# Tree attention on one core: GpSimd's V copies placed behind the next group's V loads, and stores eight groups of four heads behind the loads in place of twelve

## The chip, the core and the metric

The kernel runs on one core of a Trainium2 chip. The core has a matrix engine (TensorE, called PE in the profile), three engines for elementwise work (VectorE or DVE, ScalarE or ACT, GpSimd or POOL), an engine that mostly issues transfers (SyncE or SP), and 16 DMA engines that move data between the device memory and the core's memory SBUF. TensorE writes into a small accumulator memory, PSUM. Each engine works off its own list of instructions in order and waits on semaphores for the others.

The metric is the device time of one execution in microseconds. Beside it stands the span of a profiled execution, from its first instruction to its last, which is shorter by what lies around it.

## What is computed

```python
batch, heads, seq, dim = 8, 12, 512, 64
mask[i, i] = 1                      # and 1 at every ancestor of i
parent = i
while parent > 0:
    parent = (parent - 1) // 2
    mask[i, parent] = 1
scores = einsum('bhqd,bhkd->bhqk', Q, K) / sqrt(dim) + (1 - mask) * (-1e9)
weights = exp(scores - max(scores)); weights /= sum(weights) + 1e-10
out = einsum('bhqk,bhkd->bhqd', weights, V)
```

Each of the 512 positions is a node of a binary tree and attends to itself and to its ancestors only. There are 96 heads in all (8 x 12). Q, K, V and the output are float32, 12.58 MB each.

## The kernel before

**Tiles.** Node n = 4p + t lies in partition p, slot t. A head is then 128 partitions x 4 slots x 64 numbers. The heads are worked on at three grains: a *group* `o` of eight heads is loaded at once (12 groups, `NO`); a *pair* `i` of two heads is computed at once (48 pairs, `NP`, four to a group); four heads, a *quad* `q`, are stored at once (24 of them, `NQ`, two to a group).

**Loads.** All loads are issued by GpSimd and turn float32 into bfloat16 on the way. `load_k` and `load_q` bring the group's K and Q (line 179). `load_v_tiles(o)` issues four transfers of V: partitions 64 to 127 to a staging tile `vst`, two transfers that put partitions 32 to 63 straight into the value tile `vt` (line 197), and partitions 0 to 31 to `vst`. K, Q and `vst` have four buffers each, `vt` has four as well (`NV`).

**V's spreading.** The value tile wants rows in another order than V has them. `spread_top` (line 203) makes four copies on GpSimd, each 32 partitions by eight heads; `spread_leaves` and `spread_l7` (lines 217 and 230) copy on VectorE. `values` cannot begin with a group before its copies are made.

**A pair's way.** `transpose(i)` turns K and Q on TensorE (line 253); `evac` copies them to SBUF on VectorE (line 279). `scores1` and `scores2` multiply Q by the keys of the tree's top and of the lower parts (lines 290 to 321), with mask codes added by matmuls, and ScalarE takes the exponentials. `values(i)` multiplies by V with a column of ones beside it (line 341), and `norm(i)` divides by the sums on VectorE (lines 367 and 370) into the output tile `of[q]`. The loop over i (line 445) runs scores of pair i, values of pair i - 1, transposes of pair i + 2.

**The order on GpSimd.** It is written out by hand in `pool_program` (line 387), a generator that the main loop steps through. For groups 0 and 1 there is a start of its own with smaller loads. From group 2 on, each round issues K and Q of group o, makes the copies of group o - 1, issues V of group o, and then the two stores `2 * o - BEHIND` and the one after it, if there are such. `BEHIND` is 12, so stores begin in the round of group 6 and the last round's are quads 10 and 11. Behind the last round come the copies of group 11 and then the stores of quads 12 to 22. The last quad is stored in three pieces: two by SyncE, one by ScalarE. The stepping (line 457) settles in which order the program is written down, not when an instruction runs: GpSimd runs its list in order, held by semaphores alone. A store waits for `norm` of its two pairs. The output tiles have 15 buffers.

Of the kernel before, what the change touches and what calls it, by code (L numbers as in the profile page):

```python
# [103 lines left out]
def kernel(  # L104
# [70 lines left out]
    def load(kept, name, pool, src, o, h0=0, n=8, rows=(0, 128)):  # L175

        if o not in kept:
            kept[o] = pool.tile([P, 8, 4, D], bf16, name=name)
        nc.gpsimd.dma_start(  # L179
            out=kept[o][rows[0]:rows[1], h0:h0 + n, :, :].rearrange("p h t d -> p h (t d)"),  # L180
            in_=src[rows[0]:rows[1], 8 * o + h0:8 * o + h0 + n, :],
        )

    def load_k(o, h0=0, n=8):
        load(ksts, "kst", loads, Kr, o, h0, n)

    def load_q(o, h0=0, n=8):
        load(qsts, "qst", loads, Qr, o, h0, n)

    def load_v(o, *args):  # L190
        load(vsts, "vst", vloads, Vr, o, *args)

    def load_v_tiles(o):

        load_v(o, 0, 8, (64, 128))
        for half in range(2):
            nc.gpsimd.dma_start(
                out=vts[o % NV][32 * half:32 * half + 32, :, VCOL[1]:VCOL[1] + 2 * D],
                in_=Vr[32:64, 8 * o:8 * o + 8, 2 * D * half:2 * D * half + 2 * D],
            )  # L200
        load_v(o, 0, 8, (0, 32))

    def spread_top(o, h0=0, h1=8):
        for j in range(4):
            nc.gpsimd.tensor_copy(  # L205
                out=vts[o % NV][32 * j:32 * j + 32, h0:h1, VTOP:VTOP + D],
                in_=vsts[o][0:32, h0:h1, UNITS[TOP + j][1], :],
            )
# [168 lines left out]
    def store(eng, q, h0=0, n=4):  # L377
        eng.dma_start(  # L378
            out=Or[:, 4 * q + h0:4 * q + h0 + n, :],
            in_=ofs[q][:, h0:h0 + n, :, :].rearrange("p h t d -> p h (t d)"),  # L380
        )


    BEHIND = 12
    NO = NQ // 2

    def pool_program():

        for h0 in (0, 2):
            load_k(0, h0, 2)  # L390
            load_q(0, h0, 2)
        load_v(0, 0, 4)
        load_k(0, 4, 4)
        load_q(0, 4, 4)
        load_v(0, 4, 4)
        load_k(1, 0, 4)
        load_q(1, 0, 4)
        spread_top(0, 0, 4)
        load_v_tiles(1)
        load_k(1, 4, 4)  # L400
        load_q(1, 4, 4)
        spread_top(0, 4, 8)
        yield
        yield
        for o in range(2, NO):
            load_k(o)
            load_q(o)
            spread_top(o - 1)
            load_v_tiles(o)
            yield  # L410
            for q in (2 * o - BEHIND, 2 * o + 1 - BEHIND):
                if q >= 0:
                    store(nc.gpsimd, q)
        spread_top(NO - 1)
        for q in range(NQ - BEHIND, NQ - 1):
            yield
            store(nc.gpsimd, q)
# [17 lines left out]
    def pool_until(done, wanted):  # L435
        while done < wanted:
            next(program, None)
            done += 1
        return done

    program = pool_program()
    steps = pool_until(0, 1)
    transpose(0)
    evac(0)
    for i in range(NP + 1):
# [13 lines left out]
        else:  # L459
            steps = pool_until(steps, min(steps + 2, NO + (i - 2) // 2 - (NQ - 1 - BEHIND)))  # L460
        if i == NP - 1:
# [33 lines left out]
```

## Time and profile before

| what | value |
|---|---|
| time, three runs | 151.35, 151.4, 153.65 us; median 151.4 us |
| time of the profiled execution | 149.99 us |
| its span | 148.2 us |
| mean granted TensorE clock | 0.925 |
| busy: PE, DVE, ACT, POOL | 109.7, 96.0, 84.6, 101.7 us |
| chain of waits: PE, DVE, issue, DMA | 57%, 18%, 12%, 3% of the span |

How to read it: the profile lists instructions by line of the kernel, with their engine, operation and tiles (`vt<-vst` is a copy from the staging tile to the value tile). A time in brackets behind a row of the timeline is how long the engine had been idle, and what ended that. Rows by stretch of time give each engine's busy time and, in the last three columns, TensorE's granted clock, the DMA engines' share and the rate that they moved. The DMA share can pass 1 since the times of overlapping packets are added.

### The profile page before, as it was taken

How to read it: one execution, taken by the hardware profiler on the slowest of the kernel's cores; microseconds unless marked ns; L12 is line 12 of the kernel's file. 1: busy time of each engine (PE TensorE's matmuls, PEld its weight loads, DVE VectorE, ACT ScalarE, POOL GpSimd, SP SyncE). 2: the span in 40 equal slices, each digit the busy share in tenths (PEclk: the TensorE clock that was granted, in tenths of full speed). 3: DMA queues.
4: the chain of work that ended last, by engine and by line, in shares of the span. 5: the costliest groups of instructions: out<-in, count | busy, mean ns of one | idle time of the engine just before them, and what ended most of it. 6: DMA issues, size and time to landing. Idle time of an engine off the chain costs nothing.

```text
span 148.2 us, 5852 instructions
## 1 busy us (share of the span) xinstructions
PE 109.7 (74%) x2592; PEld 81.4 (55%) x2592; DVE 96.0 (65%) x205; ACT 84.6 (57%) x98; POOL 101.7 (69%) x155
## 2 busy tenths in 40 slices
PE   0486798988989999598689969679798697962000
PEld 0245585766867757476457747556576475741000
DVE  3037699796896987677835957748867859752000
ACT  4044258685886777667727748584586757680000
POOL 7949979449597595977975946966976907992000
PEclk9998579999999999999969999999999999998555
DMA  4999999999999999999999999999999994799993
GB/s 130 148 159 195 192 194 200 190 198 133 160 193 186 172 168 157 177 208 308 198 199 329 203 223 313 197 246 281 192 244 284 197 250 182 240 311 326 339 351 145
DMA packets 44938, 32.30 MB, mean 218 GB/s; under 512 B 7280, under 2 KB 41840, under 8 KB 44912
## 3 DMA queue, kind: packets, MB, share of 16 engines
q0 software_dynamic: 44208, 30.94, 122.4%
q1 hardware_dynamic: 560, 0.85, 1.8%
q8 instruction: 20, 0.33, 0.8%
q10 hardware_dynamic: 144, 0.13, 0.3%
q14 instruction: 6, 0.05, 0.1%
HBM read 38.21 MB, written 12.58 MB: 343 GB/s over the span
## 4 chain that ended last, share of the span: by engine, by line
PE 57%; DVE 18%; issue 12%; DMA 3%; ACT 1%; POOL 1%; ACTq 0%; POOLq 0%
PE ob L341 21%; PE kqp L253 13%; PE s L290 8%; PE s L295 5%; PE s L321 5%; DVE of L370 5%; PE s L312 4%; DVE kq L279 4%; DVE vt L217 3%; DMA qst<-in_Q_dram 3%; DVE vt L239 2%; DVE rec L367 2%; DVE vt L230 2%; POOL kst L179 1%; ACT e L326 1%
## 5 line engine op out<-in xcount | busy, mean ns | idle before, releaser
L301 ACT ACTIVATE e<-s 128x1024 bf16<-128x1024 f32 x48 | 49.2, 1024 | 44.8 <-PE s L295 43.9
L205 POOL COPY vt<-vst 32x512 bf16<-32x512 bf16 (+1 forms) x52 | 31.2, 600 | 24.9 <-DMA vst<-in_V_dram 20.7
L341 PE MATMUL ob<-vt,e 128*128 128x65 bf16 (+1 forms) x960 | 40.0, 200 | 9.2 <-issue 4.8
L326 ACT ACTIVATE e<-s 128x768 bf16<-128x768 f32 x48 | 38.6, 805 | 2.7 <-PE s L321 2.7
L341 PEld LDWEIGHTS <-e 128*128 128x128 bf16 (+1 forms) x960 | 31.5, 104 | 15.0 <-issue 6.7
L279 DVE COPY kq<-kqp 128x1024 bf16<-128x1024 bf16 x48 | 32.7, 682 | 10.1 <-PE kqp L253 10.0
L370 DVE TENSOR_TENSOR of<-ob,rec 128x512 f32<-128x512 f32 x48 | 33.2, 691 | 1.7
L253 PE MATMUL kqp<-ctile,kst 128*64 128x128 bf16 x384 | 20.8, 231 | 7.5 <-DMA kst<-in_K_dram 5.4
L367 DVE RECIPROCAL rec<-ob 128x8 f32<-128x8 f32 x48 | 9.9, 207 | 25.3 <-PE ob L341 24.5
L321 PEld LDWEIGHTS <-kq 64*128 64x128 bf16 x576 | 17.0, 96 | 10.6 <-issue 5.9
L253 PE MATMUL kqp<-ctile,qst 128*64 128x128 bf16 x384 | 20.6, 231 | 1.6 <-issue 1.3
L321 PE MATMUL s<-kq 64*128 64x96 bf16 (+2 forms) x576 | 18.3, 191 | 4.1 <-issue 4.1
L290 PE MATMUL s<-ctile 64*128 64x512 bf16 x96 | 19.8, 400 | 1.2 <-issue 1.1
L295 PE MATMUL s<-kq 64*128 64x512 bf16 x96 | 19.2, 392 | 0.7 <-DVE kq L279 0.7
L378 POOL DMA_DIRECT2D out_dram<-of x23 | 17.5, 769 | 1.4 <-issue 1.4
L253 PEld LDWEIGHTS <-kst 128*64 128x64 bf16 x384 | 13.8, 117 | 8.0 <-DMA kst<-in_K_dram 5.4
L179 POOL DMA_DIRECT2D qst<-in_Q_dram x15 | 12.8, 854 | 6.1 <-DMA qst<-in_Q_dram 2.3
L312 PE MATMUL s<-ctile 64*128 64x384 bf16 x96 | 16.8, 335 | 0.2
L253 PEld LDWEIGHTS <-qst 128*64 128x64 bf16 x384 | 14.9, 118 | 2.0 <-issue 1.4
L179 POOL DMA_DIRECT2D vst<-in_V_dram x24 | 15.9, 661 | 0.0
L179 POOL DMA_DIRECT2D kst<-in_K_dram x15 | 13.1, 873 | 0.8 <-POOLq L479 0.8
L217 DVE COPY vt<-vst 64x1024 bf16<-64x1024 bf16 (+1 forms) x26 | 12.8, 493 | 0.8
(15 smaller groups left out, 42.6 us busy)
## 6 DMA issues: line engine op xcount, KB each, us to landing
out_dram<-of POOLq DMA_DIRECT2D x23, 512.0 KB, 7.5
kst<-in_K_dram POOLq DMA_DIRECT2D x10, 512.0 KB, 8.4
qst<-in_Q_dram POOLq DMA_DIRECT2D x10, 512.0 KB, 10.0
vst<-in_V_dram POOLq DMA_DIRECT2D x13, 256.0 KB, 6.3
vt<-in_V_dram POOLq DMA_DIRECT2D x22, 64.0 KB, 6.1
vst<-in_V_dram POOLq DMA_DIRECT2D x11, 128.0 KB, 6.2
kst<-in_K_dram POOLq DMA_DIRECT2D x3, 256.0 KB, 6.9
qst<-in_Q_dram POOLq DMA_DIRECT2D x3, 256.0 KB, 7.5
```

The lines of the kernel that those rows point to most:

```text
L179: nc.gpsimd.dma_start(out=kept[o][rows[0]:rows[1], h0:h0 + n, :, :].rearrange("p h t d -> p h (t d)"), in_=src[rows[0]:rows[1], 8 * o + h0 ...
L205: nc.gpsimd.tensor_copy(out=vts[o % NV][32 * j:32 * j + 32, h0:h1, VTOP:VTOP + D], in_=vsts[o][0:32, h0:h1, UNITS[TOP + j][1], :],)
L253: nc.tensor.transpose(out=dst, in_=st[i // 4][:, 2 * (i % 4) + a, t, :], identity=perm)
L279: nc.vector.tensor_copy(out=kq[:, :, :, :].rearrange("p k (x y) c -> p k x (y c)", x=2), in_=src)
L290: nc.tensor.matmul(out=sp[:, a, :], lhsT=k1code[64 * a:64 * a + 64, :], rhs=q1code[64 * a:64 * a + 64, :], start=True, stop=False,)
L295: nc.tensor.matmul(out=sp[:, a, :], lhsT=keys(i, a, TOP), rhs=qTs[i][64 * a:64 * a + 64, :, :].rearrange("p t c -> p (t c)"), start=False, ...
L301: nc.scalar.activation(out=et[:, :, :, :].rearrange("p a t c -> p (a t c)"), in_=sp[:, :, :].rearrange("p a c -> p (a c)"), func=AF.Exp, s ...
L312: nc.tensor.matmul(out=sp[:, a, :, 32:128], lhsT=k2code[64 * a:64 * a + 64, :], rhs=q2code[64 * a:64 * a + 64, :].rearrange("p (t c) -> p ...
L321: nc.tensor.matmul(out=sp[:, a, t, lo:hi], lhsT=keys(i, a, TILE2[tile2]), rhs=qTs[i][64 * a:64 * a + 64, t, lo:hi], start=False, stop=(t, ...
L326: nc.scalar.activation(out=e2s[i % NE][:, :, :, 32:128].rearrange("p a t c -> p (a t) c"), in_=sp[:, :, :, 32:128].rearrange("p a t c -> p ...
L341: nc.tensor.matmul(out=ob[lo:hi, a, start_o:start_o + 65], lhsT=e[:, a, t, lo:hi], rhs=vt[:, 2 * (i % 4) + a, col:col + 65], **flags,)
L370: nc.vector.tensor_tensor(out=ofs[q][:, 2 * r:2 * r + 2, :, :], in0=vals, in1=rec[:, :, :, :].to_broadcast([P, 2, 4, D]), op=ALU.mult,)
```

## The change

```diff
-    BEHIND = 12
+    BEHIND = 8
     NO = NQ // 2
...
         for o in range(2, NO):
             load_k(o)
             load_q(o)
+            load_v_tiles(o)
             spread_top(o - 1)
-            load_v_tiles(o)
             yield
             for q in (2 * o - BEHIND, 2 * o + 1 - BEHIND):
                 if q >= 0:
                     store(nc.gpsimd, q)
```

In each round from group 2 on, the four transfers of group o's V are issued ahead of the four copies of group o - 1 instead of behind them. Stores begin in the round of group 4 in place of group 6; the last round issues quads 14 and 15 in place of 10 and 11. The copies of group 11 stay where they are, behind the last round, and behind them come quads 16 to 22 in place of 12 to 22. No instruction is added or taken away, and the three pieces of the last quad stay with SyncE and ScalarE.

## The prediction, written before the changed kernel ran

> **What bounds the kernel now.** I read the page's span and HBM line first, then busy time by stretches, then GpSimd's timeline, then TensorE's timeline and the chain of waits at the end.
>
> ```profile
> span 148.2 us, 5852 instructions
> HBM read 38.21 MB, written 12.58 MB: 343 GB/s over the span
> DMA packets 44938, 32.30 MB, mean 218 GB/s; under 512 B 7280, under 2 KB 41840, under 8 KB 44912
> ```
>
> Loads read four-byte numbers and leave two-byte ones: 38.21 MB read count as about half of that, and with 12.58 MB of stores they give the 32.30 MB. So GB/s is counted where the bytes land; a pure load stretch reads twice its figure. A group of eight heads loads 1.573 MB landed (3.146 MB read); a store of four heads is 0.524 MB.
>
> Busy time by stretches (after the colon: length, the five engines, clock, DMA share, GB/s):
>
> ```profile
> 21.00:31.00 10.00, 9.33 (x258) 7.28 (x254) 8.72 (x18) 7.92 (x10) 6.38 (x10) 1.00 1.48 195
> 34.00:37.00 3.00, 2.93 (x78) 2.23 (x78) 2.04 (x5) 1.59 (x2) 3.00 (x6) 1.00 0.99 118
> ...
> 21.00:63.00 42.00, 37.53 (x964) 28.46 (x960) 34.42 (x68) 30.99 (x36) 31.25 (x48) 1.00 1.38 176
> 63.00:123.00 60.00, 50.70 (x1248) 37.91 (x1244) 42.59 (x86) 39.28 (x46) 42.95 (x64) 0.97 1.37 244
> ...
> 135.25:146.30 11.05, 0.00 (x0) 0.00 (x0) 0.00 (x0) 0.00 (x0) 0.00 (x0) 0.55 0.98 331
> 146.30:148.20 1.90, 0.00 (x0) 0.00 (x0) 0.00 (x0) 0.00 (x0) 0.00 (x0) 0.50 0.06 24
> ...
> 126.00:127.00 1.00, 1.00 (x29) 0.67 (x26) 0.75 (x2) 0.37 (x1) 1.00 (x2) 1.00 0.17 53
> ...
> 126.80:146.30 19.50, 6.14 (x150) 4.56 (x146) 5.14 (x11) 5.18 (x6) 6.99 (x10) 0.74 0.98 322
> ```
>
> The last 11 us hold no arithmetic: stores drain. The reader sees three stages. Up to 63 us there are loads only, at 195 GB/s when full but 176 on average. From 63 to 123 us two stores go behind each group. From 126.8 us there are stores alone, at 322 GB/s. GpSimd's timeline says why:
>
> ```profile
> 31.48 2.75 POOL L205 COPY vt<-vst 32x512 bf16<-32x512 bf16 x4 [3.98 <-DMA vst<-in_V_dram]
> 34.18 0.69 POOL L179 DMA_DIRECT2D vst<-in_V_dram  x1
> 34.86 1.16 POOL L197 DMA_DIRECT2D vt<-in_V_dram  x2
> 36.00 0.58 POOL L179 DMA_DIRECT2D vst<-in_V_dram  x1
> 36.57 0.90 POOL L179 DMA_DIRECT2D kst<-in_K_dram  x1
> 37.44 0.91 POOL L179 DMA_DIRECT2D qst<-in_Q_dram  x1
> ...
> 110.25 0.89 POOL L179 DMA_DIRECT2D qst<-in_Q_dram  x1 [1.00 <-DMA qst<-in_Q_dram]
> 112.41 2.55 POOL L205 COPY vt<-vst 32x512 bf16<-32x512 bf16 x4 [1.27 <-DMA vst<-in_V_dram]
> ...
> 117.29 1.54 POOL L378 DMA_DIRECT2D out_dram<-of  x2
> 122.99 2.65 POOL L205 COPY vt<-vst 32x512 bf16<-32x512 bf16 x4 [4.16 <-DMA vst<-in_V_dram]
> 125.59 7.45 POOL L378 DMA_DIRECT2D out_dram<-of  x10
> ```
>
> Four copies wait for the V that landed last, and the next V loads stand behind them on the same engine: from 34 to 37 us only 118 GB/s move. At the end the last V lands at 122.99, its copies run to 125.6, then come eleven stores, whose bytes flow from 126.8 (53 GB/s on average from 126 to 127). VectorE's last instruction is the end of the arithmetic:
>
> ```profile
> 134.54 0.69 DVE of L370
> ```
>
> It ends at 135.23; the DMA queue still needs 11 us. So the end is set by when the last V lands and by how many stores are left then.
>
> **The change, part by part.**
>
> *Stores eight behind.* Groups 4 to 11 instead of 6 to 11 carry two stores each: 16 go among the loads, not 12. After the last load seven GpSimd stores and the split last one remain, eight in place of twelve. Twelve took 19.5 us (126.8 to 146.3), 1.625 us each, so eight take 13.0: **minus 6.5 us**. Their data is old enough: stores 14 and 15, issued around 112 to 118, need pairs 28 to 31, which are over by then (with four pairs to a group, group 11's first transposes, pair 44, come at 120.64 below). The 0.75 us of GpSimd that a store costs (7.45 for ten) moves with it; a group then costs GpSimd 2.65 + 0.69 + 1.16 + 0.58 + 1.54 + 0.90 + 0.91 = 8.4 us, below the 10.6 us of a group in the next rows.
>
> Price of the four stores where they go:
>
> ```profile
> 79.50:90.80 11.30, 9.60 (x245) 7.04 (x240) 8.62 (x18) 7.41 (x10) 8.25 (x13) 1.00 1.36 251
> ...
> 101.80:112.40 10.60, 9.06 (x233) 6.79 (x226) 8.30 (x17) 7.81 (x10) 8.21 (x12) 1.00 1.38 239
> ```
>
> These are groups from one V landing to the next. Loads alone at 195 GB/s need 1.573 / 195 = 8.07 us, the densest group with stores 10.6, so two stores cost 2.5 us and four **5.1 us**, all of it ahead of the last V.
>
> *Copies behind the next V loads.* The same four copies, four V issues and their order on one engine; nothing is added. What it can give back is the thin stretches: (195 - 176) / 195 x 42 = 4.1 us before 63 us. After 63 us the group of 11.3 us holds 0.7 us more than the one of 10.6. When V of a group lands now, only the next K and Q (2.1 MB read, 5.4 us at 390 GB/s) are queued, and the next V follows only after 2.65 us of copies and 2.4 us of issue. Afterwards K, Q and V (8.07 us) are queued; GpSimd needs 2.65 + 0.90 + 0.91 + 2.43 = 6.9 us for the next round, so the queue doesn't run dry. I take the 4.1 as recovered and the 0.7 as not, since there the limit told next holds in either order: **minus 4.1 us**. The ends are 0 (nothing) and 4.8 (all).
>
> A limit that stays: Q of group 11 is issued at 110.25, after a wait for a Q. These are the Q loads of groups 10 and 11 in the view of DMA issues (us to landing last), and GpSimd's row for group 10:
>
> ```profile
> qst<-in_Q_dram POOLq DMA_DIRECT2D x1, 512.0 KB, 10.2
> ...
> qst<-in_Q_dram POOLq DMA_DIRECT2D x1, 512.0 KB, 10.0
> ```
>
> ```profile
> 99.52 0.89 POOL L179 DMA_DIRECT2D qst<-in_Q_dram  x1 [1.30 <-DMA qst<-in_Q_dram]
> ```
>
> Q of group 10 went out at 99.52 and landed 10.2 later, at 109.7; Q of group 11, the eighth DMA after it, could go only then. I read this as eight GpSimd DMAs in flight at most. With two stores each part of a group then waits for its forerunner, also V's four parts, and the copies stand behind them: up to 2.4 us later than now (the V issues), at least 0. The work that hides it:
>
> ```profile
> 116.93 0.78 PE L341 MATMUL ob<-vt,e 128*128 128x65 bf16 x20 [0.53 <-DVE of L370]
> 120.64 0.39 PE L253 MATMUL kqp<-ctile,kst 128*64 128x128 bf16 x8
> 120.87 0.39 PE L253 MATMUL kqp<-ctile,qst 128*64 128x128 bf16 x8
> ```
>
> Group 10's copies end at 114.96 and its first values product starts at 116.93: 2.0 us of cover, so I take 0; at worst 0.4 us shows.
>
> *Arithmetic.* Q of group 11 lands at 120.25 and is wanted at 120.87, so 0.6 us of cover. By the sum (5.1 - 4.1) it comes 1.0 later, a wait of 0.4 us. TensorE also idles for "issue" more often once the queue is full:
>
> ```profile
> L341 PE MATMUL ob<-vt,e 128*128 128x65 bf16 (+1 forms) x360 | 14.7, 197 | 4.3 <-issue 2.9 <-DVE of L370 1.4
> ...
> L341 PE MATMUL ob<-vt,e 128*128 128x65 bf16 (+1 forms) x560 | 22.9, 199 | 3.7 <-issue 1.9 <-DVE of L370 1.8
> L321 PE MATMUL s<-kq 64*128 64x96 bf16 (+1 forms) x324 | 10.3, 189 | 4.1 <-issue 4.1
> ```
>
> The first row is 20 to 63 us, the others 63 to 135.3. Issue makes 2.9 us in 43 (0.07 per us) and at least 6.0 in 72 (0.08). If the 20 us from 43 to 63 went like the later stage, that is some tenths; I allow 1.3. The arithmetic would then end at 135.23 + 0.4 + 1.3 = 136.9. The last small stores need about 3.5 us from there: a 512 KB store on an empty queue landed in 4.7, and a quarter of it flows 1.2 us less.
>
> ```profile
> out_dram<-of POOLq DMA_DIRECT2D x1, 512.0 KB, 4.7
> ```
>
> That is 140.4, just inside the drain below; from an arithmetic end of 137.3 on, this would set the time.
>
> **Sum.** Flow of the last stores starts at 126.8 + 5.1 - 4.1 = 127.8, lasts 13.0, to 140.8; with the closing 1.9 the span is 142.7, which is 5.5 below 148.2. The profiled execution took 149.99, 1.8 around its span; the median of the runs shown, 151.4, stands 1.4 above it. On that footing: 142.7 + 1.8 + 1.4 = **145.9 us**.
>
> **The rivals.** *The gaps don't fill* (the copies' place does nothing, since V lands in the order of the queue either way). The last V is then 5.1 us late, the flow runs from 131.9 to 144.9, span 146.8, time 150.0: no change that can be told. For it: eight in flight hold in both orders. Against it: 118 GB/s from 34 to 37 us, just behind copies that waited.
>
> *Slower: TensorE starves at each group's head and its clock falls.* For it: the small cover of Q (0.6 us), and this place, where 1.91 us of idleness is followed by a lower clock:
>
> ```profile
> 72.90 1.91 issue
> 75.00:80.00 5.00, 5.00 (x101) 3.65 (x97) 2.10 (x5) 2.54 (x3) 2.44 (x4) 0.67 1.31 279
> ```
>
> To cost 2% the span must pass 151.2, so the arithmetic must end at 151.2 - 1.9 - 3.5 = 145.8, 10.6 us later: 1.5 us in each of the seven groups 5 to 11, so Q some 2.1 us later than the one before at each group. At 2 us a group: 14 us, span 135.2 + 14 + 5.4 = 154.6, time 157.8. Against it: stores cost 2.5 us per group only in groups 4 and 5, which had none; the waits show TensorE held by a load once only, at the start, though group 11's Q had 0.6 us of cover.
>
> ```profile
> PE kqp L253 <- DMA kst<-in_K_dram: 5.4, 1, 5.4
> ```
>
> *All bytes at one mean rate.* The first load's issue ends at 2.1 us:
>
> ```profile
> 1.28 0.82 POOL L179 DMA_DIRECT2D kst<-in_K_dram  x1 [0.83 <-POOLq L479]
> ```
>
> From there to 146.3 us 50.8 MB pass at 352 GB/s. If that were a ceiling over the whole, moving stores would change nothing: 151.4. Against it: 195 GB/s landed, 390 read, for ten us on end.
>
> The Trainium skill, "DMA: Bandwidth & Descriptors", section Specifications, gives a core about 358 GB/s of HBM, which speaks for this rival: as an estimate 50.8 MB take 142 us, with 2.1 before and 1.9 behind a span of 146, a time of 149. The trace disagrees with it as a ceiling for this core alone, by the 390 GB/s above.
>
> **How the numbers follow.** The forecast, with a landing of the last V between 0.3 (all gaps filled) and 3.5 us later than now, has 71%; its own range is 143.5 to 148.4 (the lower end is the arithmetic's floor, 135.2 + 3.5 + 1.9 + 3.2 = 143.8, less 0.3 for spread). Unfilled gaps 16%, starving 8%, one mean rate 5%. A measurement of this kernel can tell about 2% (148.4 and 154.4). Faster 71%, within 2% 21%, slower 8%. The range goes from 143.5 to 150.0: it takes in half of the unfilled gaps and leaves out the rest, the mean rate and starving, about 2 in 10.
>
> **What would show it.** Right: V issues directly behind Q's, 195 GB/s kept from 34 to 63 us, the last V at 123 to 125, about 13 us of stores alone, arithmetic's end at 135 to 138. Wrong: the last V at 128 (gaps not filled), waits for K, Q or V on TensorE at group heads, or an arithmetic end beyond 140, which would take over the end from the stores.

## The result and the profile after

| kernel | time, median | ratio to before, 95% interval | last V lands | arithmetic ends | span of that profile |
|---|---|---|---|---|---|
| before | 152.3 us (151.35 to 153.65) | | 122.99 | 135.23 | 148.2 |
| changed | 145.4 us (145.14 to 146.91) | 0.958 [0.948, 0.968] | 125.67 | 136.83 | 145.1 |

The changed kernel is faster by 4.2%. The ratios leave out slow executions, those more than 1.5% above the fastest of their kernel, and the medians take in all. The page of its profile begins like this:

```profile
span 145.1 us, 5866 instructions
...
GB/s 133 142 169 194 193 193 201 190 198 195 195 200 278 260 193 280 266 188 281 260 198 291 249 198 292 247 196 298 235 192 299 236 196 298 100 96 306 327 342 97
...
HBM read 38.21 MB, written 12.58 MB: 350 GB/s over the span
```

The 14 instructions more than before are none that the page counts as busy work: TensorE, VectorE, ScalarE and GpSimd have 2592, 205, 98 and 155 in both. Each of the 40 figures of the GB/s line stands for 3.6 us. From the fourth figure to the twelfth they are at 190 or more: the thin stretch is gone. Two figures of 100 and 96 near the end are lower than any that the kernel before has there. The view by stretches gives both in numbers (length, five engines, clock, DMA share, GB/s):

```profile
34.00:37.00 3.00, 2.91 (x74) 2.10 (x70) 2.53 (x6) 1.73 (x2) 2.41 (x4) 1.00 1.51 192
...
125.00:129.70 4.70, 3.15 (x92) 2.42 (x88) 4.35 (x8) 3.45 (x4) 3.90 (x6) 1.00 0.07 23
...
129.70:142.50 12.80, 4.84 (x120) 3.52 (x114) 4.19 (x9) 3.45 (x4) 3.89 (x6) 0.76 0.98 324
```

From 34 to 37 us it is 192 GB/s where it was 118. The eight stores at the end take 12.8 us where twelve took 19.5. Between the loads and these stores lie 4.7 us in which next to nothing moves. Such a gap is not new, but it has grown; the kernel before has a shorter one:

```profile
124.00:127.00 3.00, 1.94 (x55) 1.49 (x54) 2.61 (x5) 1.80 (x2) 2.92 (x5) 1.00 0.16 56
```

The timeline of GpSimd in the changed kernel says what it does then:

```profile
30.15 0.58 POOL L197 DMA_DIRECT2D vt<-in_V_dram  x1 [0.73 <-DMA vst<-in_V_dram]
30.72 0.58 POOL L179 DMA_DIRECT2D vst<-in_V_dram  x1
31.36 2.65 POOL L205 COPY vt<-vst 32x512 bf16<-32x512 bf16 x4
...
111.96 0.89 POOL L179 DMA_DIRECT2D qst<-in_Q_dram  x1 [1.93 <-PE kqp L253]
113.07 0.69 POOL L179 DMA_DIRECT2D vst<-in_V_dram  x1 [0.23 <-DMA vt<-in_V_dram]
113.75 1.15 POOL L197 DMA_DIRECT2D vt<-in_V_dram  x2
114.89 0.75 POOL L179 DMA_DIRECT2D vst<-in_V_dram  x1
115.69 2.67 POOL L205 COPY vt<-vst 32x512 bf16<-32x512 bf16 x4
118.31 1.55 POOL L378 DMA_DIRECT2D out_dram<-of  x2
125.67 2.75 POOL L205 COPY vt<-vst 32x512 bf16<-32x512 bf16 x4 [5.82 <-DMA vst<-in_V_dram]
128.38 4.46 POOL L378 DMA_DIRECT2D out_dram<-of  x6
```

V's issues now stand right ahead of the copies. The copies of the rounds no longer wait themselves: the wait has moved to the issues ahead of them. Only the last copies wait long, 5.8 us, and the seven stores behind them with them. In the kernel before, the last wait of TensorE for a load or a V copy ends at 12.39 us. In the changed one there are such waits late in the execution:

```profile
111.44 0.41 PE L253 MATMUL kqp<-ctile,qst 128*64 128x128 bf16 x8 [0.67 <-DMA qst<-in_Q_dram]
...
118.41 0.78 PE L341 MATMUL ob<-vt,e 128*128 128x65 bf16 x20 [1.53 <-POOL vt L205]
...
122.02 0.41 PE L253 MATMUL kqp<-ctile,qst 128*64 128x128 bf16 x8 [0.55 <-DMA qst<-in_Q_dram]
```

### The profile page after: what moved, and what is told of

It reads as the page before. It is cut to its first block, busy times and chain, and to the rows that moved or that the text cites. A ratio compares the mean times of both kernels' runs of the same rounds, so it can differ in the third digit from the quotient of the medians.

```text
span 145.1 us, 5866 instructions
## 1 busy us (share of the span) xinstructions
PE 108.3 (75%) x2592; PEld 80.4 (55%) x2592; DVE 97.4 (67%) x205; ACT 84.6 (58%) x98; POOL 102.3 (70%) x155
## 4 chain that ended last, share of the span: by engine, by line
PE 44%; DMA 26%; DVE 11%; issue 11%; ACT 2%; POOL 0%; POOLq 0%; ACTq 0%
PE ob L341 15%; DMA qst<-in_Q_dram 15%; PE kqp L253 11%; DMA vst<-in_V_dram 8%; PE s L290 6%; PE s L295 5%; PE s L321 4%; DVE of L370 4%; PE s L312 3%; DMA kst<-in_K_dram 3%; DVE kq L279 2%; ACT e L326 2%; DVE rec L367 1%; DVE vt L217 1%; DVE vt L239 1%
## 5 line engine op out<-in xcount | busy, mean ns | idle before, releaser
L341 PE MATMUL ob<-vt,e 128*128 128x65 bf16 (+1 forms) x960 | 39.5, 199 | 11.8 <-DVE of L370 4.8
L290 PE MATMUL s<-ctile 64*128 64x512 bf16 x96 | 19.5, 395 | 1.5 <-issue 0.8
L179 POOL DMA_DIRECT2D qst<-in_Q_dram x15 | 12.8, 850 | 11.0 <-PE s L295 4.3
L253 PEld LDWEIGHTS <-kst 128*64 128x64 bf16 x384 | 13.5, 116 | 9.8 <-DMA kst<-in_K_dram 6.0
L197 POOL DMA_DIRECT2D vt<-in_V_dram x22 | 12.8, 586 | 3.8 <-DMA qst<-in_Q_dram 1.7
## 6 DMA issues: line engine op xcount, KB each, us to landing
vst<-in_V_dram POOLq DMA_DIRECT2D x11, 128.0 KB, 9.9
```

The costliest lines, as they stand in the source:

```text
L179: nc.gpsimd.dma_start(out=kept[o][rows[0]:rows[1], h0:h0 + n, :, :].rearrange("p h t d -> p h (t d)"), in_=src[rows[0]:rows[1], 8 * o + h0 ...
L253: nc.tensor.transpose(out=dst, in_=st[i // 4][:, 2 * (i % 4) + a, t, :], identity=perm)
L290: nc.tensor.matmul(out=sp[:, a, :], lhsT=k1code[64 * a:64 * a + 64, :], rhs=q1code[64 * a:64 * a + 64, :], start=True, stop=False,)
L341: nc.tensor.matmul(out=ob[lo:hi, a, start_o:start_o + 65], lhsT=e[:, a, t, lo:hi], rhs=vt[:, 2 * (i % 4) + a, col:col + 65], **flags,)
```

## The experiments

Two theories stood at the start. The forecast's: the order of the copies fills the thin stretches, and the stores shorten the tail but put the last V off by their own time. Its rivals: the order does nothing and the stores do it all, or the arithmetic decides. All times here are in us; a ratio is to runs of the kernel before on the same chip.

| run | time | ratio, 95% interval | last V lands | arithmetic ends | span |
|---|---|---|---|---|---|
| stores only | 148.97 | 0.977 [0.970, 0.984] | 127.81 | 139.63 | 146.8 |
| order only | 146.23 | 0.958 [0.950, 0.966] | 119.18 | 135.42 | 144.5 |
| two stores ahead of the last copies | 142.62 | 0.936 [0.929, 0.942] | 123.82 | 137.00 | 140.3 |
| four behind | 146.28 | 0.959 [0.950, 0.968] | 129.37 | 141.72 | 145.0 |
| changed, again | 145.18, one run | | 123.93 | 135.35 | 143.4 |
| before, again | 150.38, one run | | 123.42 | 135.87 | 148.6 |
| stores by SyncE | 157.92 | 1.038 [1.024, 1.052] | 141.86 | 152.91 | 156.5 |
| halved loads | 148.53, one run | | 127.65 | 139.46 | 146.7 |
| four stores ahead | 142.86 | 0.944 [0.934, 0.953] | by 124.98 | 138.20 | 141.5 |
| ten behind, three ahead | 141.83 | 0.938 [0.927, 0.950] | 122.02 | 135.98 | 139.7 |

The last V's landing is the start of group 11's copies where these waited for it; the arithmetic's end is that of VectorE's last row.

**Each part alone.** In the first run only `BEHIND = 8` is set; in the second only `load_v_tiles(o)` goes ahead of `spread_top(o - 1)`, with `BEHIND = 12`.

> Only the stores move (eight quads behind); the V copies stay ahead of the next V loads. Theory: four stores cost 5.1 us among the loads, the thin stretches before the stores begin (118 GB/s at 34 to 37 us) stay thin, the tail gets 6.5 us shorter: a gain of 1.4 us, time near 150, the last V lands near 128. Rival (the place of the copies does nothing, stores alone fill the thin stretches): the same time as the full change, near 145.4, the last V near 125.7.

> Only the V copies move behind the next V loads; stores stay twelve quads behind. Theory: the load stretches are dense from the start (195 GB/s from 21 to 63 us), the last V lands 4.1 us earlier, near 119, and the twelve stores flow until 142: time near 147.3. Rival (the arithmetic's pace holds the loads back, or the order does nothing): the last V stays near 123 and the time near 151.4.

The rows of the two runs, stores only first:

```profile
34.00:37.00 3.00, 3.00 (x78) 2.24 (x78) 2.28 (x6) 1.84 (x3) 3.00 (x6) 1.00 0.88 108
...
131.60:144.40 12.80, 5.48 (x132) 4.13 (x132) 4.91 (x11) 4.64 (x6) 4.05 (x6) 0.83 0.98 322
```

```profile
34.00:37.00 3.00, 3.00 (x79) 2.13 (x74) 2.55 (x6) 1.82 (x3) 2.78 (x4) 1.00 1.52 193
21.00:63.00 42.00, 36.20 (x908) 27.02 (x910) 32.48 (x65) 29.15 (x34) 33.61 (x50) 1.00 1.48 198
...
123.00:142.30 19.30, 9.68 (x246) 7.32 (x240) 9.02 (x19) 8.45 (x10) 7.03 (x10) 0.83 0.98 324
```

The copies of group 11, which wait for the last V, in stores only and in order only:

```profile
127.81 2.65 POOL L205 COPY vt<-vst 32x512 bf16<-32x512 bf16 x4 [4.26 <-DMA vst<-in_V_dram]
```

```profile
119.18 2.55 POOL L205 COPY vt<-vst 32x512 bf16<-32x512 bf16 x4 [5.97 <-DMA vst<-in_V_dram]
```

With the order alone the load stage runs at 198 GB/s (176 before) and the last V lands at 119.18, 3.8 earlier. With the stores alone the stretch stays thin (108) and the last V lands at 127.81, 4.8 later; the eight stores take 12.8, the twelve of the order alone 19.3. The places in the trace are those of the forecast's theory, and its rivals on the order fall. In the times the order is worth more than expected: 146.2, against 147.3. Stores alone, at 149.0, beat the 150 too. The spans are nearly as worked out: 146.8 for stores alone, where 150.0 less the 3.2 that the forecast adds to a span is 146.8, and 144.5 for the order alone, where it is 144.1. What is off is the 1.4 of the 3.2 that stands for the way from the profiled execution to the median. What late loads do to TensorE stands in the rows of stores only:

```profile
81.55 0.41 PE L253 MATMUL kqp<-ctile,qst 128*64 128x128 bf16 x8 [1.82 <-DMA qst<-in_Q_dram]
...
103.44 0.41 PE L253 MATMUL kqp<-ctile,qst 128*64 128x128 bf16 x8 [2.21 <-DMA qst<-in_Q_dram]
...
114.21 0.41 PE L253 MATMUL kqp<-ctile,qst 128*64 128x128 bf16 x8 [1.46 <-DMA qst<-in_Q_dram]
```

In its waits Q holds TensorE eight times, 9.0 us in all, and the arithmetic ends at 139.6. That is the starving rival, in a small form; the order of the copies is what keeps it away in the changed kernel.

**Filling the gap before the last stores, and more stores among the loads.**

```diff
-        spread_top(NO - 1)
-        for q in range(NQ - BEHIND, NQ - 1):
+        for q in range(NQ - BEHIND, NQ - BEHIND + 2):
+            store(nc.gpsimd, q)
+        spread_top(NO - 1)
+        for q in range(NQ - BEHIND + 2, NQ - 1):
             yield
             store(nc.gpsimd, q)
```

(with the stepping of line 460 two less). The other run sets `BEHIND = 4` in the changed kernel.

> The full change, and quads 16 and 17 are stored ahead of group 11's copies instead of behind them. Theory: in the changed kernel's profile the DMA queue is empty from about 125 to 129.5 us while GpSimd waits for the last V and copies; two stores of 1.6 us fill 3.2 us of this gap: 2 to 3 us less than the full change, near 143, until the arithmetic's end (136.8 in its profile) sets the time. Rival (the arithmetic already sets the end, or the stores delay the last V): no gain, 145.4 or more.

> The full change with stores four quads behind: from group 2 on each round issues two stores, four remain for the tail. Theory: the loads were already dense, so four more stores among them put the last V off by 5.1 us (near 130.8), the arithmetic ends about as much later (near 142) and sets the end: span near 147 to 148, time near 149, slower than eight behind. Rival (the tail alone counts): 6.5 us less tail, time near 141 to 144.

Two stores ahead, by stretches:

```profile
122.00:126.00 4.00, 4.00 (x106) 2.94 (x98) 2.92 (x7) 3.33 (x4) 2.71 (x4) 1.00 1.07 385
126.00:130.00 4.00, 3.21 (x94) 2.55 (x94) 3.02 (x6) 2.79 (x4) 3.56 (x6) 1.00 0.74 264
```

The gap is filled, the last V lands at 123.82, and the time is 142.6, 2.8 below the changed kernel, as expected. Now the arithmetic, ending at 137.00, is followed by 3.3 of stores and closing, to 140.3. Four behind puts the last V off to 129.37 (130.8 expected) and the arithmetic to 141.72 (142 expected). Both are as the theory has them, but the time of 149 is missed: 146.3. Of the 2.7 in between, 2.1 lie behind the arithmetic, where 3.3 follow and 5.4 had been allowed. It had been expected slower than eight behind, and no difference can be told (0.959 against 0.958); the rival's 141 to 144 is not met either. In its waits the V copies hold TensorE seven times:

```profile
PE ob L341 <- POOL vt L205: 8.6, 7, 1.7
...
PE kqp L253 <- DMA qst<-in_Q_dram: 6.2, 8, 1.8
```

**Both kernels once more, and the limit on DMAs in flight.** The two kernels were run unaltered for a second profile. One run gives all stores to SyncE (`store(nc.sync, q)` in `pool_program`), another loads K and Q of each group in halves.

> The changed kernel once more, unaltered, for a second profile. Theory: in the profile at hand the last V's landing (125.7) is late by some 1.7 us against order alone (119.2) plus 4.8 for four stores (stores alone put it off by that), since a few DMA engines lag from 124 to 128 us at 20 to 122 GB/s; a typical execution lands near 124 and has a span near 143.5. Rival: the lag belongs to the kernel, and the second profile shows 125 to 126 again.

> The kernel before once more, unaltered, for a second profile. Its first profile (span 148.2) stands below the median of its runs. Theory: the last V lands later than 122.99 in a typical execution, by 1 to 2 us, with the tail of twelve stores unchanged at 19 to 20 us. Rival: the loads are the same and the arithmetic or the tail differs.

> The full change with all stores issued by SyncE in place of GpSimd. Theory (GpSimd has eight DMAs in flight at most, and with two stores each part of a group waits for its forerunner): six DMAs a group remain on GpSimd, so Q follows K without the idle 1 to 2.4 us ahead of it, the V parts don't wait, and the copies begin when their own V has landed; the bytes are the same, so the last V lands within 2 us of the full change's and the time is 143 to 147. Rival (Q waits for a buffer that TensorE frees, as the rows name TensorE): the idle time ahead of Q stays.

> The full change with K and Q of each group from 2 on loaded in halves, ten DMAs a group. Theory (eight in flight): less than a group is queued now; K's halves wait for the Q halves of the group before, Q's for its V parts; GpSimd's idle time ahead of K and Q grows to over 3 us a group, the V copies begin later and values wait for them: 1 to 4 us slower than the full change. Rival (each load waits for its own buffer alone): only 1.6 us of issue a group more, hidden, within 1 us of the full change.

The changed kernel's second profile, by stretches and on GpSimd:

```profile
128.00:141.30 13.30, 5.07 (x124) 3.72 (x120) 4.19 (x9) 4.57 (x6) 3.85 (x6) 0.85 0.95 314
124.00:128.00 4.00, 3.34 (x84) 2.44 (x80) 3.64 (x7) 2.60 (x4) 3.88 (x6) 1.00 0.16 58
```

```profile
123.93 2.75 POOL L205 COPY vt<-vst 32x512 bf16<-32x512 bf16 x4 [5.47 <-DMA vst<-in_V_dram]
```

The last V lands at 123.93, as the order alone plus the stores' 4.8 has it (119.18 + 4.8 = 124.0). Its time, 145.2, is near the median; the first profile, at 146.91, was the longest run of the changed kernel, and its last V was late. The wait of TensorE on V copies is not in this one. The kernel before repeats itself: last V at 123.42, and a tail of 19.5.

```profile
127.20:146.70 19.50, 6.26 (x150) 4.58 (x146) 5.52 (x12) 5.17 (x6) 7.04 (x10) 0.78 0.98 322
```

So the expectation of a later V falls, and the rival's other arithmetic or tail is not seen either (the arithmetic ends at 135.87, after 135.23). Both profiled executions of it (149.99 and 150.38) lie about 2 below the median of its runs. What its longer executions spend those 2 us on is in neither profile, and stays open.

The limit of eight DMAs in flight shows in whose landing GpSimd waits for. The waits of stores by SyncE, which leaves six DMAs a group on GpSimd, and those of the halved loads, ten a group:

```profile
POOL vt L197 <- DMA vst<-in_V_dram: 10.9, 8, 1.8
POOL vt L197 <- DMA qst<-in_Q_dram: 9.6, 3, 3.8
...
POOL vst L179 <- DMA kst<-in_K_dram: 0.9, 1, 0.9
```

```profile
POOL vst L179 <- DMA out_dram<-of: 3.3, 6, 1.5
...
POOL kst L179 <- DMA qst<-in_Q_dram: 2.8, 4, 1.3
```

Counted back in the order of issue, each of these names the eighth DMA before. With six a group, V's first straight transfer (line 197) waits for Q of the group before, the second for the first V part of the group before. With ten a group, V's last part waits for the second store of the group before, K's second half for Q's second half of the group before. A buffer of its own could not explain a V load that waits for a store. The wait ahead of Q is gone with six a group, as expected, but it has moved to V's parts, which was not. And the time is far off, 157.9 against 143 to 147. SyncE issues each store as soon as its data is there, and loads then move beside stores from 20 us on:

```profile
43.00:140.00 97.00, 73.72 (x1731) 54.54 (x1728) 61.61 (x121) 55.51 (x65) 51.30 (x77) 0.93 1.34 227
```

```profile
q0 software_dynamic: 40896, 18.88, 92.4%
q1 hardware_dynamic: 12704, 12.91, 28.8%
```

That is 227 GB/s for 97 us, against 243 in the changed kernel from 63 to 122 us, and the last V lands at 141.86, 16 to 18 later than in the changed kernel's two profiles. Part of this has the price that the forecast named: SyncE has issued 21 stores by then, where the changed kernel has put 16 among its loads, and at 5.1 for four the five more make 6.4, an estimate. The rest goes with the lower rate. The packets of SyncE's queue are of 1 KB (12.91 MB in 12,704); GpSimd's stores were about 3.6 KB each (its queue has 3,312 packets and 12.06 MB fewer without them). Whether the packet size or loads and stores running side by side costs the rate was not separated.

The Trainium skill, "DMA: Bandwidth & Descriptors", section "Issuing engines are not separate DMA queues", has it that starting transfers from several engines saves issue time only, since they all run on the same 16. Here GpSimd was spared 1.54 us of issue a group, and the kernel took 12.5 us longer than the changed one. It is the starving rival at full size: 15.0 us of TensorE's waits for Q, 8.7 for V copies, and a slower kernel.

The halved loads cost 3.3 of span against the changed kernel's second profile (146.7, 143.4) and 1.6 against its first, in one run, within the 1 to 4 expected, and as expected the V copies come later (group 10's at 119.95, after 114.08) and hold TensorE, for 13.5 us in nine waits. But GpSimd's idle time ahead of K and Q did not grow to over 3 us a group; the most in one group is 2.1, and the changed kernel's first profile has up to 2.9.

**How far it goes.** Four stores ahead at eight behind, and three ahead at ten behind.

> The full change with quads 16 to 19 stored ahead of group 11's copies (two ahead gave 142.6). Theory: with two ahead the arithmetic's end (137.0) and what follows it (3.3 us) already set the span of 140.3, so two more ahead gain nothing or cost up to 1.5 us (GpSimd issues them before the copies, and each waits for a landing): 142.5 to 144. Rival (the drain of stores still sets the end): about 1.5 us less, 141.

> V copies behind the next V loads, stores ten quads behind, quads 14 to 16 ahead of group 11's copies. Theory: two stores fewer among the loads let the last V land about 2.5 us earlier than with eight behind (near 121.5) and the arithmetic end 0 to 1.5 us earlier, while two more stores (3.2 us) drain behind: the two ends meet, 142 to 143.5, the same as two ahead at eight behind. Rival (only the arithmetic's end counts): 141 to 142.

Four ahead give nothing more, as expected. Ten behind with three ahead is at 141.8, a little below the expectation and within the rival's 141 to 142. The places are those expected: the last V at 122.02 (near 121.5) and the arithmetic's end 1.0 earlier than with two ahead. Its interval overlaps that of two ahead, so the two cannot be told apart. All three beat the kernel before. Two ahead also beats the changed kernel (0.942 at most, against 0.948 at least); the intervals of the other two overlap the changed kernel's a little.

## Why the prediction was right

The time forecast was 145.9, the median is 145.4, and the way there can be checked step by step.

- *The tail.* 1.625 a store: eight should take 13.0 and took 12.8, 13.3 and, with stores alone, 12.8. Right.
- *Four stores among the loads, 5.1.* Stores alone put the last V off by 4.8; four more, from the changed kernel's second profile (123.93) to four behind (129.37), by 5.4. From its first profile, with the late V, it is 3.7. Right.
- *The order gives back 4.1.* The order alone brought the last V forward by 3.8, and the rate between 21 and 63 us went from 176 to 198 GB/s. Right.
- *Last V 1.0 later.* 0.9 later in the second profile, 2.7 in the first, the longest run; 0.8 later with two stores ahead.
- *Flow of the last stores from 127.8 to 140.8.* From 128.0 to 141.3 in the second profile.
- *Arithmetic's end at 136.9, allowing 0.4 for Q and 1.3 for issue.* 136.83 and 135.35. The hit in the first profile is luck: Q holds TensorE for 1.2 and V copies for 1.5, where 0.4 and nothing had been allowed, and the 1.3 for issue is not there. TensorE's waits for issue come to 12.6 before and to 10.6 and 12.8 in the two profiles of the changed kernel.
- *Copies behind V's issues cost 0, at worst 0.4.* Mis-sized: 1.53 in one place of the first profile, none of it in the second, and 8.6 in seven places once more stores press (four behind). The place and the cause, V's parts waiting for their forerunners, were those named.
- *What follows the arithmetic, 3.5 + 1.9.* Mis-sized: 3.3 in all (137.00 to 140.3 with two ahead, 141.72 to 145.0 with four behind). It was not the bound in the changed kernel, so the sum did not feel it; it made the expectation for four behind too high.
- *1.4 from the profiled execution to the median.* That held for the kernel before only. Typical spans of the changed one are 143.3 to 143.7, 0.6 to 1.0 above the 142.7 of the sum, and its median stands 1.8 above them. In the second profile the 0.7 too little is 0.2 in the start of the last stores, 0.3 in their length and 0.2 in the closing (2.1 where 1.9 was taken). So two small misses cancel, and that the time is met to half a microsecond is luck; by the spans alone it is met to within 1.

Of the rivals, unfilled gaps is what stores alone show; there it gave 149.0 where 150.0 was worked out. One mean rate falls: the order alone loads 198 GB/s landed, twice that read, over 42 us, and with ten behind and three ahead the same 50.8 MB pass in a span of 139.7 us, 364 GB/s on average. That is above the 358 GB/s a core that the Trainium skill gives in "DMA: Bandwidth & Descriptors", section Specifications; the measurement decides for this core alone. Starving did not come in the changed kernel at the size of the rival, but in its neighbours. A small form of it, which the forecast had named as a sign of being wrong, is in the first profile with the 1.2 and 1.5 of waits at group heads, but the end did not hang on it: stores set it. The forecast read that a load held TensorE once only before; there is a second such wait, 0.35 for a Q at 6.39 us, also at the start.

How the gain divides is less well met. The terms give the order 4.1 and the stores 1.4 net, as they take 6.5 from the tail and give 5.1 back among the loads. In the profiled spans the order alone is worth 3.7 (148.2 to 144.5) and the stores alone 1.4 (148.2 to 146.8). But in the times the order alone already gives 146.2 and the same ratio as the whole change, 0.958, and the spans of the changed kernel's two profiles, 145.1 and 143.4, lie on both sides of 144.5. So a gain from the stores on top of the order is not shown. And in the medians each alone is worth more than its term, 6.3 and 3.5 (152.5 to 146.2 and to 149.0): the median of the kernel before lies some 2 above its profiled executions, for a reason that no profile shows, and those of the two others do not.

## What to carry to other kernels

On an engine that issues loads in order, put what must wait for data behind the issues of the next loads, not ahead of them: here that alone gave the ratio of the whole change. Moving stores among the loads only pays as far as the transfers have idle time there; where they are dense it shifts the cost and starts to starve the arithmetic; on top of the new order no gain from it is shown here. After each such gain look for the next empty stretch of the DMA engines: two stores ahead of the last wait were worth another 2.8 us.

## What the runs showed of the hardware that was not expected

- In these kernels GpSimd has at most eight DMAs in flight, whatever their kind: the waits name the eighth before with six, eight and ten a group. Whether the chip sets this limit or the way the program hands out its semaphores, no run shows.
- The same stores issued by SyncE move in packets of 1 KB in place of 3.6 KB, and the kernel is slower than before by 3.8% [2.4, 5.2]. What share of this the packets have is open.
- The last load can lag behind the rest: in the changed kernel's first profile the rate falls to 275, 122 and 60 GB/s in the three microseconds from 123 us on, and the last V lands only at 125.67. In the second it lands at 123.93. Why, no run shows.
